# DeltaNet loop of a hybrid encoder: the gate projection z0 moves between q and v0, convolutions get rank 2, and their consumers an allowance of 20

## The chip, the cores and the metric

The kernel runs on one core of a Trainium2 chip. A core has a matrix engine (TensorE, in profiles PE, with its weight loads as PEld), a vector engine (VectorE, DVE), a scalar engine (ScalarE, ACT), GpSimd (POOL) and SyncE (SP), which here issues the DMAs. Each engine works through its own queue in the order in which the program was built, and waits at semaphores for the others. The metric is the device time of one execution in microseconds (us). Before the change it is 3641.96 us, the median of 3 runs (3636.83 to 3643.74).

## The reference

A two-layer encoder on 1024 tokens of width 1024, in float32. Layer 0 mixes tokens by attention, layer 1 by a gated DeltaNet; each has a gated MLP behind it. The change is in layer 1. What that computes, cut:

```python
proj = h @ w_in                                   # 1024 -> q, k: 8 heads, v, z: 16 heads, of 128 each
qkv = silu(depthwise_conv_centred(qkv, conv_w, conv_b))     # 5 taps along the tokens
q, k = l2norm(q) * GDN_DK ** -0.5, l2norm(k)
o_fwd = chunk_gated_delta_rule(q, k, v, g_fwd, beta_fwd)
o_bwd = flip(chunk_gated_delta_rule(flip(q), flip(k), flip(v), ...))
o = rmsnorm(o_fwd + o_bwd, o_norm) * silu(z)
h = h + o @ w_out
```

The delta rule splits the tokens into chunks. For each chunk it needs a triangular inverse, which depends on k, and then a chain over the chunks, in which a state of 128x128 per head is updated step by step. The reference has chunks of 64; the kernel takes 8 chunks of 128.

## The kernel before

Every projection and MLP product is a float32 product in three parts: weights and activations are split into a high and a low part, and high x high, high x low and low x high are added (`split`, `weights`). The split of a weight tile is a cast on ACT (`wh`, L109) and a subtraction on DVE (`wl`, L110).

The DeltaNet layer is worked in eight rounds, j = 0 to 7, one for each q/k head with its two v heads. Six generators ("flows") issue the work:

- `products`: for each round six projections, each 48 matmuls of 128x512 (L489) into one of two accumulators named `mm`. In order: k, q, v0, v1, z0, z1. The rows of k, q and v are then convolved (`conv5`): one ACT instruction for the middle tap (L443), four DVE instructions for the other taps (L446), and one Silu on ACT (L447), into a tile `t`, of which there are three. The rows of z get a Silu alone (L580) and go to memory.
- `prepare`: transposes k, q and v rows on PE (L575), normalises, and computes the Gram blocks k k and q k (L546). It is the reader of the convolved tiles.
- `decays`: the decay factors, on DVE and ACT (L595 to L606).
- `inverses`: the triangular inverses, one for each round and direction (PE L659 to L754 with DVE and ACT between).
- `chains`: for each round and direction 8 chunk steps (PE L803, L804, then DVE L807, PE L822, ACT L824, PE L828 and L834, DVE L832 and L838).
- `heads_out`: normalises the output, transposes it (L870), multiplies by z.

What sets the order: on PE it is written out ahead by a small planner, the class `Weave`. It keeps a clock of its own, `now`. Each flow yields a pair (PE time that the piece takes, time until its next piece is ready) or the name of a mark that it waits for; the planner takes the first flow in its list that is ready, and `products`, the last in the list, fills what is left. A mark may carry an allowance: `self.weave.mark((name, j), 8.0)` tells that the convolved row can be read 8 units after its convolution was issued. The planner's clock doesn't know what the chip does: where the convolution is not ready in time, PE, whose order is fixed, stands still at the transposes.

On the other engines the scheduler of the framework orders the instructions when the kernel is built, by a rank: `ahead(n)` raises the rank of what is issued under it by n. The flows have 5 (chains), 4 (inverses), 3 (prepare, decays), 1 (heads_out) and 0 (products); the weight loads and splits inside `products` get 1 (`fetch`).

Of the kernel before, what the change touches and what calls it, by code (L numbers as in the profile page):

```python
# [41 lines left out]
class Trunk:  # L42
# [407 lines left out]
    def products(self, ys, tmp, begun):  # L450


        nc, w, cw = self.nc, self.ap["gdn_in"], self.cw5
        rows = [(j, n, i) for j in range(8) for n, i in (("k", 8 + j), ("q", j), ("v0", 16 + 2 * j), ("v1", 17 + 2 * j),
                                                        ("z0", 32 + 2 * j), ("z1", 33 + 2 * j))]
        parts = [(i, k) for _, _, i in rows[2:] for k in (0, 4)]
        split = []

        def fetch():
            if len(split) < len(parts):  # L460
                i, k = parts[len(split)]
                with self.ahead(1):
                    split.append(self.weights(w[i][:, k:k + 4]))

        fetch()
        for p, (j, name, i) in enumerate(rows):
            if p < 2:
                acc = begun[p]
            else:
                acc = self.big()  # L470
                for h in range(2):
                    fetch()
                    for step in self.steps(acc, split[2 * p - 4 + h], ys[4 * h:4 * h + 4], HALVES, h == 0, h == 1):
                        yield step
            if name[0] == "z":
                self.gate_rows(2 * j + int(name[1]), acc, tmp)
            else:
                self.rows[j, name] = self.conv5(acc, cw[:, i], tmp)
                self.weave.mark((name, j), 8.0)
        for step in self.first_out():  # L480
            yield step

# [1052 lines left out]
```

## Time and profile before

| | |
|---|---|
| median of 3 runs | 3641.96 us (3636.83 to 3643.74) |
| the profiled execution | 3643.63 us, of which 3641.8 us are the span from the first to the last instruction |
| busy in the span | PE 90%, PEld 73%, DVE 68%, ACT 48%, POOL 25% |
| DeltaNet rounds, 1370 to 2690 us | 1320 us: PE busy 1082.84, DVE 870.35, ACT 666.61 |
| granted PE clock in the rounds | 0.91 of full speed, against 0.97 to 0.98 in the long stretches before and behind |

In the list of waits a line says which engine waited at which instruction for which other, in total, how often, and the longest. A timeline row is start, duration, engine, line, what it writes and reads, and in brackets the idle time before it with its releaser. "L447" is line 447 of the kernel.

### The profile page before, as it was taken

To read this page: it belongs to the slowest core of one execution; us is meant where nothing else is said; L and a number is where in the kernel's file an instruction comes from. 1 tells how busy PE (TensorE), PEld (TensorE's weight loads), DVE (VectorE), ACT (ScalarE), POOL (GpSimd) and SP (SyncE) were. 2 spreads that over 40 slices of the span, in tenths; PEclk is the share of its full clock that TensorE was granted. 3 is DMA by queue.
4 is the path that set the end of the run, shared out by engine and by line. 5 is a ranking of instruction groups with operands and counts; after the bars stand their busy time and mean duration, and the time that the engine had idled before them with its cause. 6 is when DMAs were issued, how large, how long until landed. Compare 5 with 4: busy or idle time off the path is not lost. (4 is left out here: it accounts for less than half of the span.)

```text
span 3641.8 us, 54329 instructions
## 1 busy us (share of the span) xinstructions
PE 3274.0 (90%) x19690; PEld 2671.0 (73%) x19690; DVE 2478.4 (68%) x4199; ACT 1735.5 (48%) x3209; POOL 925.0 (25%) x1111
## 2 busy tenths in 40 slices
PE   7999999899999997987878887887779989999998
PEld 6877878677777875776767766666668777777876
DVE  5326887777777856677766766665663688777685
ACT  4225665445444534555554545454452454545443
POOL 1112221444440021122221223131312044444200
PEclk9999999999999998999999988998989999999999
DMA  3331116233327433233333332333344733332553
GB/s 120 102 107 52 35 58 197 96 113 102 107 76 258 141 100 101 72 98 93 110 89 101 96 99 82 95 88 93 88 139 133 255 127 107 110 102 90 189 172 110
DMA packets 249230, 410.18 MB, mean 113 GB/s; under 512 B 25473, under 2 KB 76033, under 8 KB 248961
## 3 DMA queue, kind: packets, MB, share of 16 engines
q1 hardware_dynamic: 248960, 406.71, 35.7%
q8 instruction: 155, 2.54, 0.3%
q14 instruction: 115, 0.93, 0.1%
HBM read 293.76 MB, written 107.61 MB: 110 GB/s over the span
## 5 line engine op out<-in xcount | busy, mean ns | idle before, releaser
L489 PE MATMUL mm<-base,wh 128*128 128x512 f32 x864 | 386.9, 448 | 18.4 <-DVE t L446 16.0
L110 DVE TENSOR_TENSOR wl<-w_raw,wh 128x512 fp32r<-128x512 f32 x271 | 192.7, 713 | 207.6 <-ACT wh L109 183.9
L109 ACT CAST wh<-w_raw 128x512 fp32r<-128x512 f32 x271 | 167.2, 618 | 275.4 <-PE mm L134 104.3
L153 POOL TENSOR_TENSOR rs<-rs,power 128x8 f32<-128x8 f32 (+2 forms) x38 | 66.6, 1752 | 863.1 <-DVE rs L152 863.1
L796 POOL TENSOR_SCALAR kd<-c,yds 128x128 f32<-128x128 f32 x224 | 93.1, 428 | 631.2 <-PE cp L828 446.8
L109 ACT CAST wh<-s 128x512 fp32r<-128x512 f32 x216 | 134.1, 621 | 225.9 <-PE sp L134 120.0
L109 ACT CAST wh<-a 128x512 fp32r<-128x512 f32 x164 | 101.7, 621 | 261.6 <-PE mm L134 129.4
L134 PE MATMUL sp<-base,wh 128*128 128x512 f32 (+1 forms) x672 | 210.7, 372 | 5.3 <-ACT wh L109 4.4
L575 PE MATMUL sp<-ident,t 128*128 128x128 f32 x256 | 56.2, 360 | 172.9 <-ACT t L447 172.3
L489 PEld LDWEIGHTS mm<-base,wh 128*128 128x128 f32 x864 | 168.7, 195 | 43.7 <-DVE t L446 11.3
L489 PE MATMUL mm<-base,wl 128*128 128x512 f32 x432 | 197.5, 457 | 0.0
L575 PEld LDWEIGHTS sp<-ident,t 128*128 128x128 f32 x256 | 41.0, 186 | 184.6 <-ACT t L447 178.6
L489 PE MATMUL mm<-yh,wl 128*128 128x512 f32 x432 | 175.2, 406 | 0.0
L489 PE MATMUL mm<-yl,wh 128*128 128x512 f32 x432 | 173.3, 401 | 0.9 <-DVE yl L110 0.9
L489 PE MATMUL mm<-yh,wh 128*128 128x512 f32 x432 | 174.1, 403 | 0.0
L446 DVE SCALAR_TENSOR_TENSOR t<-mm,gdn_cw,t 128x1023 f32<-128x1023 f32 (+1 forms) x128 | 163.0, 1276 | 7.7 <-ACT t L443 6.6
L110 DVE TENSOR_TENSOR wl<-s,wh 128x512 fp32r<-128x512 f32 x174 | 145.1, 835 | 24.7 <-ACT wh L109 24.2
L134 PE MATMUL sp<-base,wl 128*128 128x512 f32 (+1 forms) x432 | 157.8, 365 | 1.2 <-DVE wl L110 1.2
L134 PEld LDWEIGHTS sp<-base,wh 128*128 128x128 f32 x672 | 127.0, 189 | 27.8 <-ACT wh L109 6.9
L1124 POOL TENSOR_TENSOR s<-a,a 128x512 f32<-128x512 f32 x80 | 105.9, 1324 | 158.4 <-DVE s L1124 99.5
L1202 POOL TENSOR_TENSOR t<-t,t 128x512 f32<-128x512 f32 x66 | 102.6, 1554 | 126.4 <-DVE t L1180 124.6
L1395 POOL TENSOR_SCALAR p<-p,m 128x1024 f32<-128x1024 f32 x60 | 68.2, 1138 | 233.7 <-DVE m L1394 171.0
(535 smaller groups left out, 10269.4 us busy)
## 6 DMA issues: line engine op xcount, KB each, us to landing
a<-in_ffn_up_dram SPq DMA_DIRECT2D x160, 256.0 KB, 3.0
c<-pk SPq DMA_DIRECT2D x128, 320.0 KB, 3.0
w_raw<-in_gdn_in_dram SPq DMA_DIRECT2D x100, 256.0 KB, 2.9
g_t<-t SPq DMA_DIRECT2D x88, 256.0 KB, 2.0
raw<-g_t SPq DMA_DIRECT2D x88, 256.0 KB, 2.7
g<-t SPq DMA_DIRECT2D x66, 256.0 KB, 2.1
raw<-g SPq DMA_DIRECT2D x66, 256.0 KB, 2.9
a<-in_ffn_down_dram SPq DMA_DIRECT2D x66, 256.0 KB, 4.4
```

The costliest lines, as they stand in the source:

```text
L109: self.nc.scalar.copy(out=hi, in_=src)
L110: (engine or self.nc.vector).tensor_tensor(out=lo, in0=src, in1=hi.bitcast(F32), op=ALU.subtract)
L134: self.nc.tensor.matmul(acc if one else acc[:, hs], lhsT=a, rhs=y[:, hs], start=(first and not onto and k + t == 0), stop=(last and k == n ...
L153: nc.gpsimd.tensor_tensor(out=r, in0=v, in1=self.power[:, :w], op=ALU.pow)
L446: nc.vector.scalar_tensor_tensor(out=o, in0=a, scalar=c[:, i:i + 1], in1=o, op0=ALU.mult, op1=ALU.add)
L489: self.nc.tensor.matmul(acc[:, hs] if len(halves) > 1 else acc, lhsT=a, rhs=y[:, hs], start=(first and k + t == 0), stop=(last and k == n ...
L575: self.nc.tensor.transpose(out=pt[:, n * P:(n + 1) * P], in_=t[:, n * P:(n + 1) * P], identity=self.ident)
L796: nc.gpsimd.tensor_scalar(out=kd[:, e], in0=kn, scalar1=col(self.yds, e), scalar2=1.0, op0=ALU.mult, op1=ALU.mult)
L1124: e.tensor_tensor(out=s[i], in0=x, in1=z, op=op)
L1202: sub = lambda out, x, z: nc.gpsimd.tensor_tensor(out=out, in0=x, in1=z, op=ALU.subtract)
L1395: nc.gpsimd.tensor_scalar(out=p, in0=p, scalar1=m[:, 3:4], scalar2=1.0, op0=ALU.mult, op1=ALU.mult)
```

## The change

Three edits in `products`. The gate projection z0 is computed between q and v0, so that the order in a round is k, q, z0, v0, v1, z1. The convolution is issued under `ahead(2)`: its rank is then above the weight loads and splits (1) and heads_out (1), and below prepare and decays (3), inverses (4) and chains (5). The allowance of the mark behind it goes from 8 to 20 units of the planner's clock.

```diff
-        rows = [(j, n, i) for j in range(8) for n, i in (("k", 8 + j), ("q", j), ("v0", 16 + 2 * j), ("v1", 17 + 2 * j),
-                                                        ("z0", 32 + 2 * j), ("z1", 33 + 2 * j))]
+        rows = [(j, n, i) for j in range(8) for n, i in (("k", 8 + j), ("q", j), ("z0", 32 + 2 * j), ("v0", 16 + 2 * j),
+                                                        ("v1", 17 + 2 * j), ("z1", 33 + 2 * j))]
...
             if name[0] == "z":
                 self.gate_rows(2 * j + int(name[1]), acc, tmp)
             else:
-                self.rows[j, name] = self.conv5(acc, cw[:, i], tmp)
-                self.weave.mark((name, j), 8.0)
+                with self.ahead(2):
+                    self.rows[j, name] = self.conv5(acc, cw[:, i], tmp)
+                self.weave.mark((name, j), 20.0)
```

No arithmetic is added or taken away; what changes is the order. The lines below 478 stand one line further down in the changed kernel (L489 is L490 there, L575 is L576, and so on); L443 to L447 keep their numbers.

PE, round 6, where PE reaches the first transposes of v0 in the kernel before. `t_23792` is the convolved row of v0; `mm_23799` is the accumulator of the next projection, v1; `base3` is the fourth of its eight blocks.

```order
L828 MATMUL cp_23836<-y_23853,kd_23831 128x128 x2
L834 MATMUL cp_23850<-y_23853,pr_21941 128x128 x2
L489 MATMUL mm_23799<-base2_11451,wl_23624 128x512
L489 MATMUL mm_23799<-yh_11452,wl_23624 128x512
L489 MATMUL mm_23799<-base3_11454,wh_23623 128x512
L489 MATMUL mm_23799<-yh_11455,wh_23623 128x512
L803 MATMUL cp_23884<-st_23660,c_23877 128x256
L804 MATMUL cp_23884<-st_23660,c_23877 128x256
L575 MATMUL sp_23893<-ident_71,t_23792 128x128 x4
```

In the changed kernel the same place: `t_24082` is the convolved v0 of round 6, `mm_24089` the accumulator of v1.

```order
L710 LDWEIGHTS ah_23778
L710 MATMUL ip_24402<-tp_24378,ah_23778 32x32
L576 MATMUL sp_24437<-ident_71,t_24082 128x128 x4
L490 MATMUL mm_24089<-base6_11463,wh_24091 128x512
L490 MATMUL mm_24089<-yl_11465,wh_24091 128x512
L490 MATMUL mm_24089<-base6_11463,wl_24092 128x512
```

The transposes of v0 have moved from the fourth block of v1's projection to the seventh, and one chain step more stands before them.

The last chain step before those transposes, on PE in the changed kernel (`cp_24331` is what this step's vector instruction reads):

```order
L804 MATMUL cp_24331<-st_23672,c_24329 128x256
L805 MATMUL cp_24331<-st_23672,c_24329 128x256
L871 MATMUL sp_24341<-ident_71,o_22901 128x128 x4
L490 MATMUL mm_24089<-base5_11460,wh_24091 128x512
L490 MATMUL mm_24089<-yl_11462,wh_24091 128x512
L490 MATMUL mm_24089<-base5_11460,wl_24092 128x512
L490 MATMUL mm_24089<-yh_11461,wl_24092 128x512
L823 MATMUL cp_24352<-r0_24334,w_23649 128x128 x2
```

Of this step it stands about one block of v1's projection before the transposes.

DVE, the four taps of v0's convolution in round 6 (L446) and what stands around them, in the kernel before:

```order
L606 TENSOR_TENSOR al<-at,ah 128x512
L673 TENSOR_TENSOR w_11722<-t_11721,mask_16_11736 128x1024
L595 SCALAR_TENSOR_TENSOR pr<-pr,ebias,maskneg 128x128 x3
L446 SCALAR_TENSOR_TENSOR t<-mm,gdn_cw,t 128x1022
L446 SCALAR_TENSOR_TENSOR t<-mm,gdn_cw,t 128x1023
L602 TENSOR_TENSOR at<-pr,kks 128x512
L446 SCALAR_TENSOR_TENSOR t<-mm,gdn_cw,t 128x1023
L603 TENSOR_TENSOR pr<-pr,qks 128x512
L606 TENSOR_TENSOR al<-at,ah 128x512
L446 SCALAR_TENSOR_TENSOR t<-mm,gdn_cw,t 128x1022
```

And in the changed kernel, where these are the last three taps, and the first stands 23 instructions ahead of the first row; `r_24334` is written by the vector instruction of the chain step shown above:

```order
L808 SCALAR_TENSOR_TENSOR r_24334<-cp,negc,c 128x128 x2
L814 SCALAR_TENSOR_TENSOR o<-cp,egc,o 128x128 x2
L607 TENSOR_TENSOR al<-at,ah 128x512
L596 SCALAR_TENSOR_TENSOR pr<-pr,ebias,maskneg 128x128 x3
L446 SCALAR_TENSOR_TENSOR t<-mm,gdn_cw,t 128x1023
L603 TENSOR_TENSOR at<-pr,kks 128x512
L446 SCALAR_TENSOR_TENSOR t<-mm,gdn_cw,t 128x1023
L604 TENSOR_TENSOR pr<-pr,qks 128x512
L446 SCALAR_TENSOR_TENSOR t<-mm,gdn_cw,t 128x1022
```

Before, no chain instruction stood between v0's taps; now those of two chain steps do, and the last three taps stand behind the second of them.

## Rows read from the trace of the kernel before

**Rows 1.** The page: the span, the busy time of each engine, and three of its lines of 40 slices (busy tenths of PE and DVE, and the granted PE clock in tenths).

```profile
span 3641.8 us, 54329 instructions
PE 3274.0 (90%) x19690; PEld 2671.0 (73%) x19690; DVE 2478.4 (68%) x4199; ACT 1735.5 (48%) x3209; POOL 925.0 (25%) x1111
...
PE   7999999899999997987878887887779989999998
...
DVE  5326887777777856677766766665663688777685
...
PEclk9999999999999998999999988998989999999999
```

**Rows 2.** Stages: start and end, length, then busy us (and instructions) of PE, PEld, DVE, ACT, POOL, the granted PE clock, the DMA share and GB/s.

```profile
100.00:1100.00 1000.00, 964.69 (x4609) 785.22 (x4610) 691.70 (x947) 482.98 (x779) 315.87 (x231) 0.98 0.30 96
1370.00:2690.00 1320.00, 1082.84 (x9193) 886.01 (x9194) 870.35 (x1943) 666.61 (x1443) 304.35 (x614) 0.91 0.31 93
2690.00:2840.00 150.00, 141.24 (x971) 117.59 (x971) 77.19 (x175) 50.34 (x123) 32.41 (x71) 0.98 0.50 159
```

**Rows 3.** Waits of PE from 1370 to 2690 us: in total, times, longest.

```profile
PE sp L575 <- ACT t L447: 172.3, 21, 14.2
PE mm L489 <- DVE t L446: 16.0, 2, 11.1
PE cp L803 <- DVE st L832: 10.3, 9, 2.3
```

**Rows 4.** PE's timeline in round 6: the last two matmuls of v0's projection, the last instruction before the first transposes of v0, the transposes with their wait, and two later chain steps.

```profile
2408.94 0.40 PE L489 MATMUL mm<-base,wl 128*128 128x512 f32 x1
2409.17 0.40 PE L489 MATMUL mm<-yh,wl 128*128 128x512 f32 x1
...
2419.28 0.59 PE L804 MATMUL cp<-st,c 128*128 128x256 f32 x2
2432.61 1.12 PE L575 MATMUL sp<-ident,t 128*128 128x128 f32 x4 [12.74 <-ACT t L447]
...
2439.51 0.59 PE L803 MATMUL cp<-st,c 128*128 128x256 f32 x2
...
2445.49 0.59 PE L803 MATMUL cp<-st,c 128*128 128x256 f32 x2
```

**Rows 5.** The same stretch on DVE: the first two taps and the last.

```profile
2424.69 2.59 DVE L446 SCALAR_TENSOR_TENSOR t<-mm,gdn_cw,t 128x1022 f32<-128x1022 f32 x2
...
2430.19 1.28 DVE L446 SCALAR_TENSOR_TENSOR t<-mm,gdn_cw,t 128x1022 f32<-128x1022 f32 x1
```

**Rows 6.** On ACT: the table load and the Silu behind those taps.

```profile
2428.55 1.28 ACT L447 ACT_TABLE_LOAD   x1
2431.50 1.06 ACT L447 ACTIVATE t<-t 128x1024 f32<-128x1024 f32 x1 [1.67 <-DVE t L446]
```

**Rows 7.** The stretch from the end of v0's projection to its transposes, columns as in rows 2.

```profile
2409.90:2432.60 22.70, 9.23 (x51) 7.19 (x49) 19.90 (x41) 9.26 (x18) 8.29 (x9) 0.79 0.20 57
```

**Rows 8.** Groups of instructions from 1370 to 2690 us: count, busy us, mean ns of one, idle time before them with its releasers.

```profile
L446 DVE SCALAR_TENSOR_TENSOR t<-mm,gdn_cw,t 128x1022 f32<-128x1022 f32 (+1 forms) x123 | 156.9, 1276 | 3.9 <-ACT t L443 2.8
L443 ACT ACTIVATE t<-mm,gdn_cw 128x1024 f32<-128x1024 f32 x30 | 36.2, 1208 | 2.6 <-PE mm L489 2.4
L807 DVE SCALAR_TENSOR_TENSOR r<-cp,negc,c 128x128 f32<-128x128 f32 x196 | 58.9, 341 | 46.4 <-PE cp L804 45.8 <-PE ip L659 0.2
L813 DVE SCALAR_TENSOR_TENSOR o<-cp,egc,o 128x128 f32<-128x128 f32 x98 | 29.3, 340 | 0.0
L595 DVE SCALAR_TENSOR_TENSOR pr<-pr,ebias,maskneg 128x128 f32<-128x128 f32 x256 | 75.6, 350 | 39.5 <-DMA pr<-grow 39.3
L602 DVE TENSOR_TENSOR at<-pr,kks 128x512 f32<-128x512 f32 x64 | 44.7, 698 | 2.7 <-ACT pr L597 2.0
L603 DVE TENSOR_TENSOR pr<-pr,qks 128x512 f32<-128x512 f32 x64 | 44.3, 693 | 0.6
L606 DVE TENSOR_TENSOR al<-at,ah 128x512 f16<-128x512 f32 x64 | 44.7, 699 | 11.3 <-ACT ah L605 10.8
L870 PE MATMUL sp<-ident,o 128*128 128x128 f32 x112 | 20.1, 308 | 2.9 <-ACT h L566 2.8
```

**Rows 9.** Four stretches at the lower clock, each behind a wait of PE; columns as in rows 2.

```profile
2535.50:2545.70 10.20, 3.43 (x36) 2.60 (x37) 4.80 (x16) 5.12 (x12) 0.00 (x0) 0.50 0.03 8
2607.20:2620.90 13.70, 2.79 (x10) 2.40 (x11) 9.68 (x16) 4.79 (x6) 0.00 (x0) 0.50 0.08 26
2422.90:2436.60 13.70, 3.99 (x15) 3.60 (x16) 9.23 (x13) 5.01 (x7) 0.00 (x0) 0.50 0.12 40
2463.80:2477.50 13.70, 6.89 (x42) 6.13 (x42) 4.77 (x6) 4.37 (x6) 0.12 (x1) 0.50 0.28 86
```

**Rows 10.** The projection's matmuls alone in an unbroken stretch: busy us of PE (count) and of PEld, clock, DMA.

```profile
2826.00:2837.50 11.50, 11.50 (x52) 9.39 (x50) 1.00 0.70 222
```

**Rows 11.** The two halves of a weight split from 1370 to 2690 us, columns as in rows 8.

```profile
L110 DVE TENSOR_TENSOR wl<-w_raw,wh 128x512 fp32r<-128x512 f32 x92 | 63.7, 693 | 80.6 <-ACT wh L109 57.4 <-PE mm L489 11.9 <-ACT t L719 4.4
L109 ACT CAST wh<-w_raw 128x512 fp32r<-128x512 f32 x92 | 56.7, 617 | 53.2 <-PE mm L489 51.7 <-DMA c<-pk 1.0
```

## The prediction

> **What bounds the kernel now.** I read the page first: PE is busy 90% of the span, DVE 68%, so matmuls carry the kernel; but in the middle of the slices PE falls to 7 and 8 tenths, and the granted clock dips in the same slices [rows 1]. The stages place this in the DeltaNet rounds: of 1320 us PE is idle 1320 - 1082.84 = 237 us, at a clock of 0.91, while the long stretch before runs at 96% and 0.98 [rows 2]. The list of waits names the cause: 172.3 of the 237 us are 21 waits of the transposes (L575) for the Silu at the end of a convolution (L447), at most 14.2 us each; the next cause is 16.0 [rows 3]. So what bounds the rounds is a latency: PE's order is fixed, and it reaches the reader of a convolved row too early.
>
> Round 6 shows one. v0's projection ends at 2409.17 + 0.40 = 2409.57, and PE has filled its time up to 2419.28 + 0.59 = 2419.87: a cover of 10.3 us. The transposes start at 2432.61: the convolution needed 23.0 us, and PE stood for 12.7 [rows 4]. Its own work is 1.21 us on ACT, four taps of 1.28 on DVE and the Silu of 1.06, 7.4 in all [rows 6, 8]. The rest is queueing: its first tap starts only at 2424.69, and in the whole stretch DVE is busy 19.9 of 22.7 us with other flows' work [rows 5, 7]. Whoever makes the cover longer gets the wait back as far as DVE can follow.
>
> **The change part by part.**
>
> The allowance of 20. The planner now puts the reader later. In round 6 there stand between v0's projection and its transposes 38 projection matmuls, three chain steps and some pieces of the inverses and of heads_out. A chain step with what is woven around it takes 2445.49 - 2439.51 = 6.0 us on PE [rows 4]; three are 18, and what goes beyond (two matmuls at 11.50/52 = 0.22, eight transposes of heads_out at 20.1/112 = 0.18, some 1.8 for inverse pieces) brings the cover to about 22. Counted the same way, the covers of rounds 1 to 7 go from 8 to 16 us to 19 to 30. All the work is the old work, so PE gains nothing else and loses nothing else; the last projection and the tail behind the rounds stand where they stood.
>
> For k, v1 and q that is enough. Their waits are part of the 21, which have 172.3/21 = 8.2 us each on average [rows 3]; with 10 to 13 us more cover, and a need that does not grow, they go. This is hidden behind projection matmuls and chain steps; without that cover they would come back whole.
>
> For v0 it is not enough by itself, because the vector order there has changed. Two chain steps now stand between its taps; the last three taps wait behind the vector instruction of the third chain step after v0's projection. From there to the last tap DVE has two L807 (0.68), two L813 (0.68), one L606 (0.70), three L595 (1.05), three taps (3.83), one L602 and one L603 (1.39): 8.3 us [rows 8]. Then comes the Silu: today the transposes start 2432.61 - (2430.19 + 1.28) = 1.1 us behind the last tap [rows 4, 5], the table load being done while ACT waits [rows 6]. PE has about 5 us from that chain step to the transposes: less than one 6.0 us step, since its last part is missing. Shortage 8.3 + 1.1 - 5 = 4.4 us if DVE is up to date at that step; in the odd rounds one more piece of the chain stands between, and it is about 2. The other end is a DVE that never catches up in this chain: from the chain's second step to the last tap it has 90 instructions, 42 us by their mean durations, against five chain steps (30 us) and about 5 us more on PE: 42 + 1.1 - 35 = 8, and 10 with a table load in the open. I take 6.5, nearer the upper end, since rows 7 show DVE nearly full there. The same count leaves a shortage at seven places: v0 in rounds 3 to 7, k and v1 in round 2. 7 x 6.5 = 46 us (15 to 70). So 172 - 46 = 126 us of waiting go.
>
> The clock. Behind a long wait PE runs at the lower level (1.2 instead of 2.4 GHz, 0.50 in the rows): four such stretches have 3.43, 2.79, 3.99 and 6.89 us of PE work in them, 4.3 on average, of which half, 2.1 us, is lost [rows 9]. 21 waits become 7: 14 x 2.1 = 30 us come back. The Trainium skill, "TensorE: Matmul & The Clock Gate", section "HAM oscillation — how this bites in real kernels", puts the penalty at half of the throttled time; here that would be half of the 10 to 14 us of a stretch, but most of a stretch is the wait itself, so the rows' smaller number stands.
>
> The rank of 2. It lifts the taps above the weight splits and heads_out, not above the flows that fill DVE. The splits that now stand behind taps need 0.62 + 0.69 us [rows 11] and have a half row of 24 matmuls, at least 24 x 0.22 = 5.3 us [rows 10], before PE asks; I cost them at nothing, and the first rival is what it costs if that cover is gone.
>
> z0 between q and v0. It moves 48 matmuls, a Silu, its store to memory and two weight loads on SP ahead of v0's; the DMA engines are used at 0.31 there [rows 2]. It spreads convolution work over more PE time. No cost; a store that holds SP would show at the weight splits.
>
> What is late next. PE's other waits, 237 - 172 = 65 us today, meet a DVE that gets less rest: 870 us of work in about 1180 instead of 1320 us, 74% instead of 66% [rows 2]. None of the rows shows this state; it costs from nothing to another 65. I take 20, since 74% leaves room on average and only the chains are tight.
>
> Sum: 126 + 30 - 20 = 136 us less than the profiled execution's 3643.6: 3507.6. That execution is 1.7 us above the median, so 3506. Ends: 157 + 35 - 0 = 192 gives 3450, 102 + 20 - 65 = 57 gives 3585.
>
> **The rivals.**
>
> Slower: the weight splits give way. Place: the first matmul of a half row (L489) behind a convolution. If a split waits for a whole convolution, 1.21 + 4 x 1.28 = 6.3 us, it comes 6.3 + 1.3 - 5.3 = 2.3 us late, at two half rows behind each of 28 convolutions: 56 x 2.3 = 129 us, about the gain. From 136/56 = 2.4 us a half row it decides; with the other vector work of a full stretch ahead of it, 4 us, it is 224, and the time 3506 + 224 = 3730. For it: DVE is the tight engine. Against: PE has no such wait in rows 3, and splits wait for PE, not PE for them (51.7 us of idle time before L109) [rows 11].
>
> DVE becomes the bound: v0's places at the upper end and the other waits doubled: 172 - 70 + 20 - 65 = 57, 3585. For it rows 7, against it the 34% idle of DVE over the rounds.
>
> The accumulators. v1's accumulator is needed again by the next round's k about 14 us after v1's projection, where it had 17 or more; should the taps end 18 us behind it as v0's do (2431.47 - 2409.57 = 21.9) [rows 4, 5], PE waits at L489 for L446 some 4 to 8 us a round, seven rounds: 28 to 56, time about 3548. Today that wait is 16.0 in two cases [rows 3]. The Trainium skill, "Perfetto Trace Analysis", section "Identifying the Most-Contended Engine", has a rule for it: the same gap again and again can mean that SBUF or PSUM has no room for the next tile. By that rule an allowance would only move the gap; rows 3 name a Silu, not a buffer, so it gets a small chance.
>
> The full gain: no shortage left at v0, all of 172 + 44: 3426. For it: the 4.4 was worked out for the worst-placed row. Against: DVE's full stretch.
>
> No effect: the planner's new order makes other readers as late as it makes these early; 3642. Against: the order of PE shows the covers doubled.
>
> **How the numbers follow.** Forecast 0.52; DVE bound 0.17; accumulators 0.13; full gain 0.07; slower 0.06; no effect 0.05. The time is the forecast's, 3506; its own range is 3465 to 3550. To hold 8 in 10 the range takes in the two smaller gains and leaves out full gain, slower, no effect and a little: 3455 to 3600. Within 0.2% (7 us, about what a measurement of this kernel can tell from no change) I put 0.05, faster by more 0.89, slower by more 0.06.
>
> **What would show it.** Right: in the rounds the waits of L576 for L447 fall from 172 to 20 to 80 us, the longest at v0 and below 10; the rounds' granted clock rises to 0.95 or more; waits of L490 for L110 stay near nothing. Wrong: waits at L490 for L110 or L446 of tens of us; waits of the chain (L804 for L833) well above 10; or as many waits for L447 as before, with v0's longer.

## The result, and the profile after

The changed kernel takes 3546.88 us, the median of 4 runs (3530.72 to 3549.61), against 3639.39 for the kernel before on the same chip. The ratio is 0.9737, with a 95% interval of 0.9705 to 0.977: faster by 2.6%, inside the range, 41 us above the predicted 3506. Of the page of its profiled execution, the lines that answer to [rows 1]:

```profile
span 3545.4 us, 54292 instructions
PE 3263.7 (92%) x19690; PEld 2649.4 (75%) x19690; DVE 2478.2 (70%) x4199; ACT 1732.9 (49%) x3212; POOL 922.7 (26%) x1111
...
PE   7999999799999998897898978989889989999998
...
PEclk9999999999999999998999989999899989999999
```

The work is the same (19690 matmuls, DVE busy 2478.2 us against 2478.4); the span is 96.4 us shorter, and PE's dents in the middle are shallower, not gone. For an account of these 96.4 us the span is cut at the last matmul of L489 (L490 in the changed kernel); what lies ahead of the cut is called the projection stage. The stages of the kernel before, with columns as in [rows 2]:

```profile
1370.00:2838.00 1468.00, 1222.08 (x10156) 1002.04 (x10156) 946.31 (x2115) 715.57 (x1562) 336.76 (x685) 0.91 0.33 100
2838.00:3641.80 803.80, 758.23 (x3412) 614.45 (x3410) 598.14 (x776) 376.69 (x609) 231.57 (x163) 0.97 0.43 139
```

And of the kernel after:

```profile
1370.00:2735.00 1365.00, 1206.06 (x10153) 975.36 (x10152) 945.20 (x2114) 712.87 (x1565) 334.06 (x685) 0.94 0.35 107
2735.00:3545.40 810.40, 761.38 (x3412) 617.21 (x3412) 599.15 (x776) 377.75 (x610) 231.83 (x163) 0.96 0.43 138
```

PE's idle time in the projection stage falls from 1468 - 1222.08 = 245.9 us to 158.9, its busy time by 16.0, and the rest of the kernel grows by 6.6. The waits of PE in that stage, the answer to [rows 3] (in total, times, longest):

```profile
PE sp L871 <- POOL o L863: 49.9, 19, 11.9
PE sp L576 <- DVE z L872: 26.2, 11, 3.8
PE sp L576 <- ACT t L447: 20.5, 3, 7.8
PE mm L490 <- DVE t L446: 10.7, 1, 10.7
PE sp L871 <- DVE z L872: 8.0, 2, 6.1
...
PE sp L871 <- DVE kks L549: 2.0, 2, 1.0
```

In the kernel before, the same transposes (there L870) have two lines in the answer to the same question, from 1370 to 2838 us:

```profile
PE sp L870 <- ACT h L566: 2.8, 5, 0.8
...
PE sp L870 <- DVE z L871: 0.6, 1, 0.6
```

The wait for the Silu (L447) has fallen from 172.3 us to 20.5. At the top stands a wait that the kernel before hardly had: the transposes of `heads_out` (L871) for the last step of its normalisation on POOL (L863). All waits at L871 come to 49.9 + 8.0 + 2.0 = 59.9 us, before to 3.4. Round 6 of the changed kernel shows what it is. PE:

```profile
2354.01 0.39 PE L490 MATMUL mm<-yh,wl 128*128 128x512 f32 x1
...
2370.93 0.59 PE L805 MATMUL cp<-st,c 128*128 128x256 f32 x2
2383.46 0.47 PE L871 MATMUL sp<-ident,o 128*128 128x128 f32 x1 [11.93 <-POOL o L863]
...
2385.68 0.77 PE L490 MATMUL mm<-base,wh 128*128 128x512 f32 x1
...
2390.55 0.88 PE L710 MATMUL ip<-tp,ah 32*32 32x32 f16 x32
2394.19 0.63 PE L576 MATMUL sp<-ident,t 128*128 128x128 f32 x4 [2.76 <-DVE z L872]
```

DVE in the same stretch (the third chain step, the last taps of v0, then the normalisation):

```profile
2372.21 0.60 DVE L808 SCALAR_TENSOR_TENSOR r<-cp,negc,c 128x128 f32<-128x128 f32 x2
...
2374.63 1.28 DVE L446 SCALAR_TENSOR_TENSOR t<-mm,gdn_cw,t 128x1023 f32<-128x1023 f32 x1
...
2378.22 1.27 DVE L446 SCALAR_TENSOR_TENSOR t<-mm,gdn_cw,t 128x1022 f32<-128x1022 f32 x1
2379.41 0.15 DVE L859 TENSOR_TENSOR ss<-ss,rq 128x8 f32<-128x8 f32 x1
...
2382.69 0.17 DVE L861 TENSOR_TENSOR ro<-ro,rq 128x8 f32<-128x8 f32 x1 [1.76 <-POOL ro L153]
```

The last step of the normalisation on POOL:

```profile
2383.03 2.81 POOL L863 TENSOR_SCALAR o<-o,ro 128x128 f32<-128x128 f32 x8 [0.37 <-DVE ro L861]
```

And v0's Silu on ACT:

```profile
2379.53 1.06 ACT L447 ACTIVATE t<-t 128x1024 f32<-128x1024 f32 x1 [2.85 <-DVE t L446]
```

v0's projection ends at 2354.01 + 0.39 = 2354.40. PE works on to 2370.93 + 0.59 = 2371.52 and then reaches the transposes of `heads_out`, whose input is not normalised: the first small DVE instruction of that (L859) runs only at 2379.41, 7.9 us later and right behind v0's last tap. From there the normalisation passes between DVE and POOL, and after another 4.05 us PE has its first block. PE has stood for 11.93 us when it goes on at 2383.46. It reaches v0's own transposes at 2390.55 + 0.88 = 2391.43; v0's Silu ended at 2380.59, and what PE still waits for there is the `sp` bank (L872). So v0 is as late as ever, 26.2 us behind its projection; another reader, which stands ahead on PE, pays for it.

### The profile page after: what moved, and what is told of

It is laid out like the page before. It is cut to its first block, busy times and chain, and to the rows that moved or that the text cites. A ratio compares the mean times of both kernels' runs of the same rounds, so it can differ in the third digit from the quotient of the medians.

```text
span 3545.4 us, 54292 instructions
## 1 busy us (share of the span) xinstructions
PE 3263.7 (92%) x19690; PEld 2649.4 (75%) x19690; DVE 2478.2 (70%) x4199; ACT 1732.9 (49%) x3212; POOL 922.7 (26%) x1111
## 5 line engine op out<-in xcount | busy, mean ns | idle before, releaser
L490 PE MATMUL mm<-base,wh 128*128 128x512 f32 x864 | 389.3, 451 | 15.3 <-DVE t L446 14.8
L110 DVE TENSOR_TENSOR wl<-w_raw,wh 128x512 fp32r<-128x512 f32 x271 | 191.6, 710 | 196.2 <-ACT wh L109 174.6
L490 PEld LDWEIGHTS mm<-base,wh 128*128 128x128 f32 x864 | 168.2, 195 | 40.4 <-issue 15.3
L490 PE MATMUL mm<-base,wl 128*128 128x512 f32 x432 | 193.8, 449 | 0.0
L490 PE MATMUL mm<-yh,wl 128*128 128x512 f32 x432 | 174.4, 404 | 0.0
L446 DVE SCALAR_TENSOR_TENSOR t<-mm,gdn_cw,t 128x1023 f32<-128x1023 f32 (+1 forms) x128 | 163.0, 1276 | 15.0 <-ACT t L443 14.4
L490 PE MATMUL mm<-yl,wh 128*128 128x512 f32 x432 | 173.4, 401 | 0.2
L490 PE MATMUL mm<-yh,wh 128*128 128x512 f32 x432 | 173.4, 401 | 0.0
L110 DVE TENSOR_TENSOR wl<-s,wh 128x512 fp32r<-128x512 f32 x174 | 145.5, 837 | 25.9 <-ACT wh L109 25.5
L110 DVE TENSOR_TENSOR gl<-raw,gh 128x512 fp32r<-128x512 f32 x132 | 97.2, 737 | 31.9 <-ACT gh L109 31.6
L110 POOL TENSOR_TENSOR wl<-s,wh 128x512 fp32r<-128x512 f32 x42 | 75.2, 1790 | 168.3 <-ACT wh L109 168.3
```

Source lines behind the costliest of these rows:

```text
L110: (engine or self.nc.vector).tensor_tensor(out=lo, in0=src, in1=hi.bitcast(F32), op=ALU.subtract)
L446: nc.vector.scalar_tensor_tensor(out=o, in0=a, scalar=c[:, i:i + 1], in1=o, op0=ALU.mult, op1=ALU.add)
L490: self.nc.tensor.matmul(acc[:, hs] if len(halves) > 1 else acc, lhsT=a, rhs=y[:, hs], start=(first and k + t == 0), stop=(last and k == n ...
```

## The experiments

Two theories first. A: the gain is the longer cover on PE, from the allowance alone. B: it comes from where the convolutions stand on DVE, by the place of z0 and by the rank. Each part was run alone. "Latency" in what follows is the time from the last matmul of a projection to the end of its Silu, worked out from the trace, the mean over rounds 1 to 7; before it is 19.3 us for v0 and for v1, and 16.4 over k, q, v0 and v1. Differences between runs are of medians; the kernel before varied by 7 us between the sets of runs, and by the ratios the steps against the whole change come out about 10 us less favourable.

**z0 alone.**

```diff
-        rows = [(j, n, i) for j in range(8) for n, i in (("k", 8 + j), ("q", j), ("v0", 16 + 2 * j), ("v1", 17 + 2 * j),
-                                                        ("z0", 32 + 2 * j), ("z1", 33 + 2 * j))]
+        rows = [(j, n, i) for j in range(8) for n, i in (("k", 8 + j), ("q", j), ("z0", 32 + 2 * j), ("v0", 16 + 2 * j),
+                                                        ("v1", 17 + 2 * j), ("z1", 33 + 2 * j))]
```

> Only z0 moves between q and v0; allowance 8 and rank 0 as before. Theory A (the gain is PE's longer cover behind a convolution, which the allowance makes): the covers stay near 10 us, so the transposes wait for the Silu of L447 as before, 150 to 175 us in the rounds, and the time stays within 20 us of 3640. Theory B (the gain comes from spreading the convolutions, or from their rank): the order alone brings a third of the 93 us or more, below 3610.

Measured: 3599.56 us, ratio 0.9908 (0.9887 to 0.9929). Waits of PE in its projection stage:

```profile
PE sp L575 <- ACT t L447: 117.0, 20, 12.0
PE sp L575 <- DVE z L871: 16.3, 7, 4.4
PE sp L870 <- POOL o L862: 12.7, 8, 7.6
```

The wait for the Silu falls by 55 us without any longer allowance: v1's latency falls from 19.3 to 13.5 us, and 7 x 5.8 = 41 is most of it. v0's own latency rises, from 19.3 to 20.9. The time is what B asked for, and A alone is wrong. Already here a new wait of `heads_out` appears (L870). In rounds 3 and 5 it stands just ahead of v0's transposes, so a part of the 55 us has only changed its place.

**The allowance alone**, 12 in place of 8. No run has the whole 20 in the old order.

```diff
-                self.weave.mark((name, j), 8.0)
+                self.weave.mark((name, j), 12.0)
```

> Only the allowance is changed, from 8 to 12, in the old order and at rank 0. Theory A: each of the 21 waits gets 4 us more cover, 21 x 4 = 84 at most, less at the short ones: L447 waits fall to about 100 us and the time to 3570 (3550 to 3600). Theory B: the waits move to other readers, 3640 within 20.

Measured: 3603.13 us, 0.9919 (0.9899 to 0.9939).

```profile
PE sp L575 <- ACT t L447: 132.6, 17, 15.3
PE mm L489 <- DVE t L446: 26.9, 3, 15.0
```

v0's latency rises from 19.3 to 22.3 us and the mean from 16.4 to 18.7: part of what the allowance adds in cover the convolution takes back, and the accumulators (L489) wait 11 us more. Both expectations missed: the waits for L447 did not fall to 100 us, and the time is outside either range.

**The rank alone.**

```diff
-                self.rows[j, name] = self.conv5(acc, cw[:, i], tmp)
+                with self.ahead(2):
+                    self.rows[j, name] = self.conv5(acc, cw[:, i], tmp)
```

> Only the rank of 2 for the convolutions. Theory A: the taps stay behind the chains, inverses and decays, so L447 waits stay at 140 us or more; what they overtake (weight splits, heads_out) is late instead; 3640 within 25. Theory B: the waits for L447 fall by half or more, 3590 or below.

Measured: 3605.70 us, 0.9927 (0.9908 to 0.9947), v0's latency 18.5.

```profile
PE sp L576 <- ACT t L447: 151.1, 20, 13.1
```

A had the waits right and the time too high, by 9 us; B had neither. Alone, the place of z0, an allowance of 12 and the rank are worth 27 to 33 us each, and the whole change 93.

**All but the rank**, on the changed kernel.

```diff
-                with self.ahead(2):
-                    self.rows[j, name] = self.conv5(acc, cw[:, i], tmp)
+                self.rows[j, name] = self.conv5(acc, cw[:, i], tmp)
```

> All of the change but the rank: z0 moved, allowance 20, convolutions at rank 0. PE's order is that of the changed kernel. In the changed kernel PE waits 50 us for the normalised output of heads_out (L871 for POOL L863), whose vector work stands right behind v0's last tap. Theory T1 (heads_out is late because the convolutions outrank it): these waits fall below 15 us and the time below 3530. Theory T2 (DVE is late there with chain, inverse and decay work, and whatever reads first shows the wait): the wait goes back to the name L576 for L447, about the same size, and the time is 3547 within 15, or above.

Measured: 3536.16 us, 0.9733 (0.9712 to 0.9754): no different from the whole change. PE's order is the same in both. In round 6:

```profile
2373.71 0.47 PE L870 MATMUL sp<-ident,o 128*128 128x128 f32 x1 [6.25 <-POOL o L862]
...
2389.69 1.12 PE L575 MATMUL sp<-ident,t 128*128 128x128 f32 x4 [7.78 <-ACT t L447]
```

6.25 + 7.78 = 14.0 us, where the whole change has 11.93 + 2.76 = 14.7 at the same two places. Over the stage, waits for L447 and waits of `heads_out` together are 39.7 + 36.0 = 75.7 us, against 20.5 + 59.9 = 80.4. The rank decides mainly which reader's name the shortage carries. T1 asked for waits of `heads_out` below 15 us; it stands above the convolutions here and still waits 32.1 us for L862, so T1 is at most a part. T2 had the time, but only a part of the wait went back to L447. Three explanations were carried on. T1: `heads_out` is late because convolutions outrank it. T2: DVE as a whole is late, full of chain, inverse and decay work, and whoever reads first shows it. T3: the taps of v0 are split by chain steps, and it would help to have them together.

**heads_out at rank 3, above the convolutions**, on the changed kernel.

```diff
-                                (self.heads_out(dp), 1), (self.products(ys, tmp, begun), 0)):
+                                (self.heads_out(dp), 3), (self.products(ys, tmp, begun), 0)):
```

> The changed kernel with heads_out at rank 3 instead of 1, above the convolutions; PE's order is the same. T1 (rank): its waits (L871 for POOL L863, 50 us in the changed kernel) fall below 20 us, time 3525 or below. T2 (DVE is late with chain, inverse and decay work): heads_out's vector instructions come only some 3 us earlier in each round, its waits stay at 30 us or more and what they lose v0 gains; 3547 within 12.

Measured: 3518.76 us, 0.9688 (0.9671 to 0.9705).

```profile
PE sp L871 <- POOL o L863: 37.1, 16, 9.1
```

T1 had the time and T2 the wait. T1 has a share, 28 us by the medians and (0.9737 - 0.9688) x 3640 = 18 by the ratios, but not the whole.

**Convolutions above everything**, rank 6 in place of 2.

```diff
-                with self.ahead(2):
+                with self.ahead(6):
```

> The changed kernel with the convolutions at rank 6, above all flows; PE's order is the same. The four taps of v0 stand within two chain instructions of each other. T2: the same DVE work still has to be done before heads_out's transposes and the chain steps, so L447 waits fall below 10 us but L871 waits stay at 30 us or more and waits of the chain (L804 for L833, L823 for L808) rise by 10 us or more; 3547 within 20. T3 (the taps' split is what makes the place late): 3515 or below.

Measured: 3575.49 us, 0.9837 (0.9821 to 0.9853), 29 us slower than rank 2. All convolutions now take 9.7 us and the wait for L447 is gone, but:

```profile
PE sp L871 <- POOL o L863: 33.3, 19, 7.7
PE sp L576 <- DVE z L872: 32.5, 11, 5.1
PE ip L660 <- DVE x L695: 21.7, 8, 3.9
PE cp L823 <- DVE r L808: 11.7, 17, 1.1
```

The inverses (L660) and the chains (L823) now wait for vector work behind the taps. T3 falls: together and early is worse. T2 had the names of the waits, but its time (3547 within 20) was too low by 8 us; the waits of L804 for L833, which it named too, stay at 3.9 us.

**The decays below the convolutions**, rank 1 in place of 3.

```diff
-            for flow, ahead in ((self.chains(dp), 5), (self.inverses(dp), 4), (self.prepare(tmp, dp), 3), (self.decays(dp), 3),
+            for flow, ahead in ((self.chains(dp), 5), (self.inverses(dp), 4), (self.prepare(tmp, dp), 3), (self.decays(dp), 1),
```

> The changed kernel with decays at rank 1 instead of 3; PE's order is the same. In a round some 10 us of decay work leave the stretch of DVE before v0's last tap and go behind it. T2: the waits at that place (L871 for POOL, L576 for L447 and for z, 97 us in the changed kernel) fall to 60 or below, time 3520 (3500 to 3535). If the decays' own reader is the tight one, the waits go to L747 and L660 of the inverses instead and the time is 3547 or above.

Measured: 3528.88 us, 0.9707 (0.9688 to 0.9726). No wait for L447 is left and v0's latency is 16.6 us, but `heads_out` waits longer:

```profile
PE sp L871 <- POOL o L863: 66.1, 24, 12.2
```

T2 had the time, not the waits: with 24.0 us of L576 for L872 they are 90 us, where 60 or below was expected. `heads_out` still stands below the convolutions.

**Both: decays 1 and heads_out 3.**

```diff
-            for flow, ahead in ((self.chains(dp), 5), (self.inverses(dp), 4), (self.prepare(tmp, dp), 3), (self.decays(dp), 3),
-                                (self.heads_out(dp), 1), (self.products(ys, tmp, begun), 0)):
+            for flow, ahead in ((self.chains(dp), 5), (self.inverses(dp), 4), (self.prepare(tmp, dp), 3), (self.decays(dp), 1),
+                                (self.heads_out(dp), 3), (self.products(ys, tmp, begun), 0)):
```

> Both: decays at rank 1 and heads_out at rank 3. T2: heads_out's vector work comes some 10 us earlier in each round, between v0's taps; its waits fall below 20 us, v0's may stay; time 3505 (3485 to 3525). T1: as with heads_out's rank alone.

Measured: 3486.34 us, 0.9594 (0.9578 to 0.9611): 60 us less than the whole change (52 by the ratios), and the fastest of all. Its stage and its waits:

```profile
1370.00:2677.00 1307.00, 1201.74 (x10153) 971.74 (x10151) 947.57 (x2114) 702.74 (x1561) 340.32 (x685) 0.96 0.36 112
```

```profile
PE sp L576 <- DVE z L872: 24.2, 10, 5.1
PE ip L660 <- DVE w L674: 20.0, 14, 10.1
PE sp L871 <- POOL o L863: 17.2, 20, 3.1
```

DVE in its round 6, the same place as above (v0's last two taps and the normalisation between them):

```profile
2330.37 0.16 DVE L859 TENSOR_TENSOR ss<-ss,rq 128x8 f32<-128x8 f32 x1
2330.45 1.27 DVE L446 SCALAR_TENSOR_TENSOR t<-mm,gdn_cw,t 128x1023 f32<-128x1023 f32 x1
...
2336.90 0.17 DVE L861 TENSOR_TENSOR ro<-ro,rq 128x8 f32<-128x8 f32 x1
2336.99 1.28 DVE L446 SCALAR_TENSOR_TENSOR t<-mm,gdn_cw,t 128x1022 f32<-128x1022 f32 x1
```

PE's order is unchanged, DVE's work is unchanged (947.57 us); what moved is that L596 to L607 are ranked behind taps and normalisation. No wait of PE names a line of the decays, but they pay a little: L660 waits for L674, the first vector work of an inverse, which reads what the decays made, and that wait has grown from 7.0 to 20.0 us. T2 holds, with the decays as the part that could move. The ranks order ACT, POOL and SP too; that DVE's order is what counts is read from the rows of round 6, and no run isolates it. The idle time of PE is 105.3 us.

**The same without the rank over the weight splits**: convolutions 0, decays -1, heads_out 1.

```diff
-                with self.ahead(2):
-                    self.rows[j, name] = self.conv5(acc, cw[:, i], tmp)
+                self.rows[j, name] = self.conv5(acc, cw[:, i], tmp)
...
-            for flow, ahead in ((self.chains(dp), 5), (self.inverses(dp), 4), (self.prepare(tmp, dp), 3), (self.decays(dp), 3),
+            for flow, ahead in ((self.chains(dp), 5), (self.inverses(dp), 4), (self.prepare(tmp, dp), 3), (self.decays(dp), -1),
```

> The convolutions' own rank goes back to 0 and the decays go to -1, so that the decays stand below the convolutions and heads_out (1) again, as in the run with decays 1 and heads_out 3, but weight splits (1) stay above the convolutions. Theory D (only who stands ahead of the taps and of heads_out on the vector engine counts; the rank over the weight splits is worth nothing): 3486 +-15. Rival R (the rank 2 itself counts once the decays are out of the way): 3510 or more, with the transposes waiting for convolved rows again (more than 30 us for L447).

Measured: 3488.61 us, 0.9607 (0.959 to 0.9623), as fast as the run before it, L870 waiting 16.4 us. D holds: the weight splits neither lose nor gain by it.

**The ranks alone, on the kernel before** (old order, allowance 8; convolutions 2, decays 1, heads_out 3).

```diff
-                self.rows[j, name] = self.conv5(acc, cw[:, i], tmp)
+                with self.ahead(2):
+                    self.rows[j, name] = self.conv5(acc, cw[:, i], tmp)
...
-            for flow, ahead in ((self.chains(dp), 5), (self.inverses(dp), 4), (self.prepare(tmp, dp), 3), (self.decays(dp), 3),
-                                (self.heads_out(dp), 1), (self.products(ys, tmp, begun), 0)):
+            for flow, ahead in ((self.chains(dp), 5), (self.inverses(dp), 4), (self.prepare(tmp, dp), 3), (self.decays(dp), 1),
+                                (self.heads_out(dp), 3), (self.products(ys, tmp, begun), 0)):
```

> The kernel before, in its order and with its allowance of 8, with rank 2 for convolutions, decays 1 and heads_out 3. Theory D: the convolutions' latency falls by some 4 us (v0 to about 16), so the 172 us of waits for L447 fall to about 100, time about 3570. Rival C (the ranks are worth something only with the longer cover): 3600 or more, waits above 130 us.

Measured: 3559.56 us, 0.9797 (0.9782 to 0.9811). Three numbers in the ranks bring 75 us, most of what the whole change brings, and PE's order is that of the kernel before:

```profile
PE sp L576 <- ACT t L447: 86.7, 20, 9.1
PE ip L660 <- DVE w L674: 27.0, 16, 3.8
```

The latency of v0 falls from 19.3 to 12.3 us, the wait for L447 to half. The forecast of D was 3570 and 100 us.

**A later heads_out**: decays 1, heads_out 3, and its own allowance 20.

```diff
-                yield 0.0, 16.0
+                yield 0.0, 20.0
```

> Decays 1 and heads_out 3 on the changed kernel, and heads_out's own allowance from 16 to 20, so that its transposes come one chain step later. If what is left of their waits (L871 for L863, 17 us in 20 waits) is a cover too short by 1 to 3 us, it falls below 8 us and the time to 3475 to 3486. If the shortage only moves on to the next reader of the vector engine, as it has done so far: 3486 +-8 with the waits elsewhere.

Measured: 3505.84 us, 0.9651 (0.9637 to 0.9666), 20 us slower than without it. What L871 gains, others lose:

```profile
PE sp L576 <- DVE z L872: 29.3, 10, 7.9
...
PE sp L871 <- POOL o L863: 8.5, 12, 1.8
PE sp L576 <- POOL o L863: 8.3, 1, 8.3
```

Neither expectation fits: the waits did move, as the second said, but at a price of 20 us. Of it 17 are idle time of PE in the stage (122.1 against 105.3) and 6 stand behind it.

**A shorter allowance**: decays 1, heads_out 3, allowance 14.

```diff
-                self.weave.mark((name, j), 20.0)
+                self.weave.mark((name, j), 14.0)
```

> Decays 1 and heads_out 3 on the changed kernel, and the allowance 14 in place of 20. If the long cover is still needed once the vector engine serves the taps earlier: waits of L576 for L447 10 to 40 us, 3495 to 3515. If the ranks alone have cut the latency below what 14 covers: 3486 +-8 and no such waits.

Measured: 3501.51 us, 0.9638 (0.9624 to 0.9652), L576 waiting 14.2 us for L447 in 6 waits, as the first expectation said. The long cover is still worth 15 us when the ranks are right.

PE in the projection stage of the main runs, in us (idle: the stage's length less PE's busy time):

| run | time (ratio) | v0's latency | idle | at transposes for L447 | at heads_out's | other |
|---|---|---|---|---|---|---|
| before | 3639.39 | 19.3 | 245.9 | 172.3 | 3.4 | 70.2 |
| ranks alone | 3559.56 (0.9797) | 12.3 | 169.1 | 86.7 | 5.7 | 76.7 |
| the change | 3546.88 (0.9737) | 22.5 | 158.9 | 20.5 | 59.9 | 78.5 |
| change, rank left out | 3536.16 (0.9733) | 27.4 | 149.2 | 39.7 | 36.0 | 73.5 |
| change, decays 1, heads_out 3 | 3486.34 (0.9594) | 16.9 | 105.3 | 0 | 19.2 | 86.1 |

## Why the prediction was right, and where it was not

The direction, the place and the mechanism were right: PE's covers grew, the wait for L447 went, and the gain stayed short of the whole 172 us because DVE does not follow. The size was not. Term by term, out of the stages and waits above:

| term | forecast | measured |
|---|---|---|
| waits for L447 | -126 | 20.5 - 172.3 = -151.8 |
| PE's other waits in the stage | +20 | (158.9 - 20.5) - (245.9 - 172.3) = +64.8 |
| clock, as PE's busy time | -30 | 1206.06 - 1222.08 = -16.0 |
| behind the stage | 0 | 810.4 - 803.8 = +6.6 |
| sum | -136 | -96.4 |

The errors partly cancel: 26 us more than forecast came back at L447, and 65 less in the other terms. That the time still lies 41 us from the forecast owes something to luck.

**The seven places.** All were found. k and v1 of round 2 and v0 of round 3 are the three waits left for L447, 6.93, 5.86 and 7.75 us, on average 6.8 where the prediction took 6.5. At v0 of rounds 4 to 7 the wait stands at L871 instead, 11.94, 11.33, 11.93 and 11.33 us. So the seven cost 20.5 + 46.5 = 67 us, not 46, inside the bound of 70. In round 6 the cover is 17.1 us up to `heads_out` and 2390.55 + 0.88 - 2385.68 = 5.75 behind its four transposes: 22.9, as counted. The last tap ended 2379.49 - 2372.21 = 7.3 us behind the third chain step's vector instruction (8.3 forecast).

**The step that failed** is the sentence that the cover holds "eight transposes of heads_out at 20.1/112 = 0.18". They were counted as work that fills PE's time, at their duration, and not asked what they wait for. They are readers of the same full DVE, in round 6 they stand about 6 us ahead of v0's transposes, and their normalisation starts behind the same taps. With that, a shortage of a few us at v0 becomes one of 11 to 12 at L871. It is the reader that comes first, not the one whose allowance was changed, that sets the wait. This is most of the miss of the second term: +56.5 of its +64.8 are waits at L871. The prediction let that term cost "from nothing to another 65" and took 20; it came out at the upper end, for a reason that the prediction did not have.

**z0: "No cost".** It is no cost but a gain of 33 us of its own, mostly at v1, that the sum doesn't have. What it is that makes v1 faster was not isolated. "It spreads convolution work over more PE time" was the right sentence without its number.

**The rank 2 at nothing** was right for the change as a whole (no difference when it is left out), though for another reason than given: it is worth 27 us in the kernel before, and here it only passes the shortage from v0 to `heads_out`. The weight splits lose nothing by it; L490 hardly waits for L110, and the slower rival didn't come.

**The clock** rose from 0.91 to 0.94, not to 0.95. Long waits remain under another name (of L871 four are above 11 us), and behind the one in round 6 PE runs slower again: the L490 row at 2385.68 takes 0.77 us, the one at 2354.01 took 0.39. The trace's record of the granted clock has 257.3 us at 0.50 (1.2 instead of 2.4 GHz) in the projection stage before and 151.7 after. PE was busy in 134.8 us of them before and in 85.9 after. Half of that work is what the lower level costs: (134.8 - 85.9) / 2 = 24 us came back, near the forecast 30. The sum of PE's busy time fell by only 16.0; counted at full clock it is 8 us longer under the new order, and why is open. The prediction's argument that most of a low stretch is waiting holds for the four stretches of [rows 9], where PE is busy a third of the time, and not for the stage, where it is busy 134.8 of 257.3 us. The Trainium skill, "TensorE: Matmul & The Clock Gate", section "HAM oscillation — how this bites in real kernels", puts the penalty at half of the throttled time. By that rule (257.3 - 151.7) / 2 = 53 us would have come back, an estimate; the trace's 24 is less than half of it.

**Two readings.** Of the 19.9 us that DVE is busy in [rows 7], 5.1 are v0's own four taps, so other flows' work is 14.8 us and not all of it. And q, which the prediction counts among the 21 waits, had none before: they stand at k, v0 and v1.

**The rivals.** DVE as the bound comes nearest in its reason. Both its conditions look met: 67 us at the seven places (70 assumed) and 64.8 at the other waits (65). But the 46.5 us at L871 stand in both, so its sum charges them twice. And DVE has 945 us of work in 1365: not its load counts but the order in it, as the ranks show. The accumulators' price, 3548, is nearest to the measured time, by chance, since its mechanism did not come. The accumulators were no loss: L490 waits 10.7 us for L446, once, where L489 waited 16.0. The chain waits (L804 for L833) stay below 10, as forecast. A buffer does show up elsewhere: L576 waits 26.2 us for L872, which reads the one `sp` bank that this stage has. It stays at 17 to 33 us in all runs with the whole new order of PE. The Trainium skill, "Perfetto Trace Analysis", section "Optimization Strategy", says that a gap that repeats can mean that the next tile has no room. That is the rule that the prediction cites for the accumulators, under the heading of another section of the page; the 11 waits for L872 fit it better than the one for L446. A second `sp` bank was not tried, so what it is worth is open.

## What to carry to other kernels

Where one engine's order is fixed ahead and another works through a full queue, count for each reader, not only for the one that is changed, how far behind its input's producer it stands and what is queued ahead of that producer; the first reader pays. Before a wait is covered by moving its reader, look for work in the producer's queue that nobody waits for soon: here two numbers (decays behind, the normalisation ahead) were worth 50 to 60 us on top of the change, and with the convolutions' rank as a third 75 us without the rest of it. Raising the late work above all else is not the same thing (29 us worse): then the inverses and the chains wait.

## What was not expected of the hardware

Nothing of an instruction's duration changed: the taps take 1276 ns before and after. What was new is how little the mean granted clock of a stage tells: with convolutions at rank 6 the stage has 1224.97 us of PE busy time at a granted clock of 0.94, and the whole change 1206.06 at the same 0.94. That mean counts waits like work. At 0.50 the stage has 163.9 us with rank 6, in 123.0 of which PE is busy, and 151.7 us with 85.9 in the whole change. Half of the difference in work is 18.5 us, and the busy times differ by 18.9. So it is the work that falls into the low stretches that counts, not their share of the time.
